# The opening and the close of a hybrid decoder layer: the norm's weights in four row tiles, filler matmuls, an earlier x tile, an earlier scale

## The chip, the core and the metric

The kernel runs on one core of a Trainium2 chip. The core has five engines that work at the same time: TensorE (PE, matmuls and transposes, writes to PSUM), VectorE (DVE), ScalarE (ACT), GpSimd (POOL) and SyncE (SP, which mostly issues transfers). The metric is the device time of one execution in microseconds (us).

## The reference

One layer: RMS norm of x (512 rows of 1024), one input projection, eight heads of block-sparse attention beside eight heads of a chunked gated delta rule, an output projection, and a squared-ReLU MLP, with a norm ahead of and behind each half. What the change touches is the first norm with the projection, and the last norm:

```
def rms_norm(x, w):
    xf = x.astype(jnp.float32)
    y = xf * lax.rsqrt(jnp.mean(xf * xf, axis=-1, keepdims=True) + EPS)
    return (y * w.astype(jnp.float32)).astype(x.dtype)
...
h = rms_norm(x, pre_mix_norm[l])
proj = jnp.einsum('bsd,dc->bsc', h, w_in[l])
...
x = x + rms_norm(mix, post_mix_norm[l])
h = rms_norm(x, pre_mlp_norm[l])
m = jnp.einsum('bsf,fd->bsd', jnp.square(jax.nn.relu(jnp.einsum('bsd,df->bsf', h, w_up[l]))), w_down[l])
x = x + rms_norm(m, post_mlp_norm[l])
```

The sum of the scan's heads runs over chunks of 64 rows and needs the inverse of a triangular matrix for each; the kernel computes it in blocks of 32 and merges them.

## The kernel before

**Numbers in two parts.** Most products are made of three matmuls: an operand is split into a rounded part (hi, a cast on ACT) and the rest (lo, a subtraction on DVE or POOL), and hi·hi, hi·lo and lo·hi are added up (`mm3`, line 141; `split`, line 109; `ended`, line 132, for weights). Plain float32 matmuls, which are slower, are used for transposes (`transpose`, line 80), for the norm's weights and in the scan.

**Order.** TensorE's instructions stand in an order that a planner in the program writes out. Generators (`pre_norm`, `projections`, `scan` and others) yield either the name of a mark or a waiting time, and the class `Weave` (line 28) runs the one of the lowest rank whose time has come. Its clock `now` goes forward with each matmul by the columns that it streams (`mm`, line 76). The waiting times stand in the table `WAIT` (line 20), the times at which x tiles may be transposed in `START` (line 24). The plan's clock only orders instructions; on the chip they wait by semaphores. During the first norm ACT, DVE and POOL keep program order too (line 190), and in the MLP SP as well.

**The opening.** `pre_norm` (line 187) takes x in four tiles of 128 rows. Tile by tile: ACT squares and sums a row (line 214), POOL makes the reciprocal root (`rstd_of`, line 167, two instructions), DVE multiplies x by the root and by the norm's weights (line 220), TensorE transposes the result in 8 blocks (line 231), and ACT and DVE split it into `hT_h` and `hT_l`. The norm's weights have to stand in all 128 partitions: they are loaded as one row of 1024 (line 200), and two matmuls with a column of ones (line 209) spread them over two PSUM banks `nb`, from which DVE reads them.

SP issues in this order: x tile 0, the norm's row, x tile 1, two blocks of projection weights, x tile 2, two blocks more, x tile 3, and small constants. POOL issues the identity matrix that the transposes need (line 201).

`ahead` steps the generator `projections` (line 249): its first two steps issue the loads of the weights of the first two items, its third splits the first item's. After tiles 0 and 1 the sum of squares and the scaling of tiles 2 and 3 follow on ACT, POOL and DVE (lines 235 to 241), with the split of the second item's weights between them. Then the first two items' matmuls for tiles 0 and 1 run, 24 each (line 272), then the transposes of tiles 2 and 3.

**PSUM.** There are eight banks in three groups: two `mm`, three `g`, three `a` (line 156). A new tile of a group takes the bank that has been free longest, and its first writer waits until the tile before it has had its last read. The first two projection items take the two `mm` banks (line 262).

**The middle.** When the triangular inverses are done (mark `inverse`, line 732), `scan` (line 735) is put into the plan. It issues eight transfers that bring the inverses' blocks back (lines 742 and 745), yields `WAIT["merge"]`, and then puts its first matmuls (32x32 tiles, line 754) into TensorE's order, between those of the projection. Behind the projections come the weights of the output projection (line 895).

**The close.** In the MLP's down projection the last eight steps are run for one tile at a time (line 1387). For each, `half` (line 1309) squares and sums the second half row on ACT and multiplies it by the norm's weights on DVE (line 1320); then `finish` (line 1329) calls `normed_y` (line 1324: a small addition on DVE, the root on POOL), multiplies by the root, adds x (line 1336) and issues the stores.

## Time and profile before

| | us |
|---|---|
| runs, median (lowest to highest) | 658.01 (657.56 to 658.2) |
| profiled execution, its own time | 657.88 |
| its span, first to last instruction | 656.1 |

The span is 1.8 us shorter than the execution's own time. The profile shows one execution. "Busy" is the time in which an engine had an instruction running; PE is TensorE's matmuls and PEld its weight loads, which overlap them. A timeline row gives the start, the duration, the engine, the line of the program, what is written and read with its shape, how many instructions the row merges, and in brackets how long the engine had been idle and what ended that. The chain of waits is followed back from the last instruction, at each step to what released it. A line can be a helper's: line 77 is every matmul, line 81 every transpose, and 134, 135, 110 and 111 are the halves of a split.

### The profile page before, as it was taken

To read this page: it belongs to the slowest core of one execution; us is meant where nothing else is said; L and a number is where in the kernel's file an instruction comes from. 1 tells how busy PE (TensorE), PEld (TensorE's weight loads), DVE (VectorE), ACT (ScalarE), POOL (GpSimd) and SP (SyncE) were. 2 spreads that over 40 slices of the span, in tenths; PEclk is the share of its full clock that TensorE was granted. 3 is DMA by queue.
4 is the path that set the end of the run, shared out by engine and by line. 5 is a ranking of instruction groups with operands and counts; after the bars stand their busy time and mean duration, and the time that the engine had idled before them with its cause. 6 is when DMAs were issued, how large, how long until landed. Compare 5 with 4: busy or idle time off the path is not lost.

```text
span 656.1 us, 11128 instructions
## 1 busy us (share of the span) xinstructions
PE 630.3 (96%) x4357; PEld 523.6 (80%) x4357; DVE 445.9 (68%) x643; ACT 358.9 (55%) x602; POOL 180.5 (28%) x215
## 2 busy tenths in 40 slices
PE   7899989989999999989999999999999999999995
PEld 4788767766677777668899899999998888887884
DVE  4358676897522364566455678888879888988775
ACT  6366463364646656744332576566565656665661
POOL 4356655422446234002402132111111230000002
PEclk9999999989999999999999999999999999999998
DMA  7132313223251202482278998999889999957503
GB/s 241 61 100 79 81 65 104 98 77 125 96 114 50 67 34 81 135 274 105 97 303 230 234 250 195 233 274 283 241 233 335 322 295 290 287 194 291 194 1 128
DMA packets 60225, 113.16 MB, mean 172 GB/s; under 512 B 15700, under 2 KB 34644, under 8 KB 59790
## 3 DMA queue, kind: packets, MB, share of 16 engines
q1 hardware_dynamic: 42446, 83.03, 36.3%
q0 software_dynamic: 17728, 29.43, 21.6%
q8 instruction: 34, 0.56, 0.4%
q14 instruction: 17, 0.14, 0.1%
HBM read 106.65 MB, written 35.15 MB: 216 GB/s over the span
## 4 chain that ended last, share of the span: by engine, by line
PE 82%; DVE 8%; DMA 6%; ACT 2%; issue 1%; POOL 1%; SPq 0%; DVEq 0%; POOLq 0%; ACTq 0%
PE ps_mm L77 43%; PE ps_g L77 22%; PE ps_a L77 14%; DMA w_raw<-in_w_out 3%; PE ps_a L81 2%; PE ps_g L81 1%; DVE inv L726 1%; DVE conv L346 1%; DVE pr L725 1%; DMA xx<-in_x 1%; DMA xy<-d_x 1%; DMA wd<-d_T 1%; DMA inv<-d_n 1%; DVE wo_l L123 1%; POOL rkq L172 0%
## 5 line engine op out<-in xcount | busy, mean ns | idle before, releaser
L135 POOL TENSOR_TENSOR w_lo<-w_raw,w_hi 128x512 fp32r<-128x512 f32 x54 | 70.6, 1308 | 119.2 <-ACT w_hi L134 111.3
L77 PE MATMUL ps_mm<-hT_h,w_hi 128*128 128x512 f32 (+1 forms) x224 | 94.0, 420 | 1.0 <-DVE conv L346 1.0
L77 PE MATMUL ps_mm<-hT_h,w_lo 128*128 128x512 f32 (+1 forms) x224 | 87.3, 390 | 0.0
L77 PE MATMUL ps_mm<-hT_l,w_hi 128*128 128x512 f32 (+1 forms) x224 | 87.2, 389 | 0.0
L110 ACT CAST wdh<-wd 128x1024 fp32r<-128x1024 f32 x53 | 55.8, 1053 | 52.2 <-PE ps_mm L77 23.6
L111 DVE TENSOR_TENSOR u_l<-w,u_h 128x1024 fp32r<-128x1024 f32 x46 | 56.2, 1224 | 36.0 <-ACT u_h L110 35.4
L111 DVE TENSOR_TENSOR wdl<-wd,wdh 128x1024 fp32r<-128x1024 f32 x53 | 64.9, 1225 | 22.9 <-ACT wdh L110 22.7
L110 ACT CAST u_h<-w 128x1024 fp32r<-128x1024 f32 x46 | 47.8, 1046 | 55.6 <-PE ps_a L77 20.7
L1133 POOL DMA_DIRECT2D d_T<-in_w_down x32 | 33.0, 1032 | 144.5 <-DMA d_T<-in_w_down 84.2
L134 ACT CAST w_hi<-w_raw 128x512 fp32r<-128x512 f32 x56 | 34.6, 619 | 42.6 <-PE ps_mm L77 17.1
L77 PEld LDWEIGHTS ps_mm<-hT_h,w_hi 128*128 128x128 f32 x224 | 43.1, 193 | 14.5 <-issue 7.2
L77 PEld LDWEIGHTS ps_mm<-hT_h,w_lo 128*128 128x128 f32 x224 | 43.1, 192 | 9.0
L168 POOL TENSOR_SCALAR s<-s 128x1 f32<-128x1 f32 x12 | 3.8, 317 | 167.5 <-DVE s L1326 108.6
L77 PEld LDWEIGHTS ps_mm<-hT_l,w_hi 128*128 128x128 f32 x224 | 43.3, 193 | 6.2 <-DVE hT_l L111 0.2
L77 PE MATMUL ps_mm<-wdh,u_h 128*128 128x512 f32 x116 | 45.3, 390 | 0.0
L77 PE MATMUL ps_mm<-wdl,u_h 128*128 128x512 f32 x116 | 45.2, 389 | 0.0
L77 PE MATMUL ps_mm<-wdh,u_l 128*128 128x512 f32 x116 | 45.1, 389 | 0.0
L346 DVE SCALAR_TENSOR_TENSOR conv<-ps_mm,cw,conv 128x511 f32<-128x511 f32 (+2 forms) x36 | 26.8, 744 | 12.5 <-ACT conv L343 12.1
L111 DVE TENSOR_TENSOR u_l<-f,u_h 128x1024 fp32r<-128x1024 f32 x28 | 34.1, 1219 | 0.0
L77 PE MATMUL ps_g<-wdh,u_h 128*128 128x512 f32 x80 | 31.2, 390 | 0.4 <-DVE y L1307 0.4
L77 PE MATMUL ps_g<-wdh,u_l 128*128 128x512 f32 x80 | 31.1, 389 | 0.0
L77 PE MATMUL ps_g<-wdl,u_h 128*128 128x512 f32 x80 | 31.1, 389 | 0.0
(428 smaller groups left out, 1725.8 us busy)
## 6 DMA issues: line engine op xcount, KB each, us to landing
d_T<-in_w_down POOLq DMA_DIRECT2D x48, 512.0 KB, 10.9
wd<-d_T SPq DMA_DIRECT2D x32, 512.0 KB, 6.2
w<-in_w_up SPq DMA_DIRECT2D x28, 512.0 KB, 8.0
w_raw<-in_w_in SPq DMA_DIRECT2D x54, 256.0 KB, 2.6
wd<-in_w_down SPq DMA_DIRECT2D x24, 512.0 KB, 8.1
w_raw<-in_w_out SPq DMA_DIRECT2D x16, 256.0 KB, 2.8
d_T<-d_T POOLq DMA_DIRECT2D x8, 512.0 KB, 11.9
xx<-in_x SPq DMA_DIRECT2D x4, 512.0 KB, 6.5
```

The lines of the kernel that those rows point to most:

```text
L77: nc.tensor.matmul(o, l, r, **kw)
L81: nc.tensor.transpose(o, i, ident[:k, :k])
L110: nc.scalar.copy(hi, src)
L111: tt(lo, src, f32(hi), op=OP.subtract)
L123: (sub or tt)(lo, raw, f32(hi), op=OP.subtract)
L134: nc.scalar.copy(hi, raw)
L135: (sub or tt)(lo, raw, f32(hi), op=OP.subtract)
L168: nc.gpsimd.tensor_scalar(r, ss, 1.0 / n, EPS, op0=OP.mult, op1=OP.add)
L346: stt(c[:, s:], p[:, :512 - s], cw[:, ft, j:j + 1], c[:, s:], op0=OP.mult, op1=OP.add)
L725: tt(v, iN[:, 0:m, m:m + 1].to_broadcast([128, m, w]), iU[:, m:m + 1, m:32].to_broadcast([128, m, w]), op=OP.mult)
L726: tt(iU[:, 0:m, m:32], iU[:, 0:m, m:32], v, op=OP.subtract)
L1133: nc.gpsimd.dma_start(d_T[t][k], block(b, second)[k], accum_op=OP.add, max_dma_last_dim=1024)
```

## The change

- The norm's weights are loaded as four rows of 256, into partitions 0, 32, 64 and 96, and spread by four matmuls of one row each at four row positions of the array, into four banks: three `a`, one `mm`. DVE's scaling of a tile becomes four instructions of 256 columns instead of two of 512.
- `busy(n)` puts n float32 matmuls of 128 columns on a tile of ones into TensorE's order, which write to the other `mm` bank and are read by nobody: six ahead of the norm's weights, five behind them, two between the transposes of tiles 0 and 1.
- SP issues the identity matrix, behind x tile 1 and ahead of the projection's weights, instead of POOL.
- At the close, `normed_y` is called for tiles 0 and 1 right behind the last sum of squares, ahead of the product with the norm's weights.
- `WAIT["merge"]` is 11.0 instead of 10.

```
-WAIT = {... 'merge': 10, ...}
+WAIT = {... 'merge': 11.0, ...}
+FILL = (6, 5, 2)
...
     def pre_norm(ahead):
-        one = tmp("one")[:1, :128]
-        nc.vector.memset(one, 1.0)
+        ones = tmp("one")
+        nc.vector.memset(ones[:, :128], 1.0)
...
-        nrow = nb0[:1]
         sqs = big("xs0", (128, 2, 1024))
-        nb = [bank("a") for _ in range(2)]
+
+        nb = [bank("a"), bank("a"), bank("a"), bank("mm")]
+        idle = bank("mm")
+
+        def busy(n):
+            for _ in range(n):
+                mm(idle[:, :128], ones[:, :128], ones[:, :128], start=True, stop=True)
...
         take(0)
-        nc.sync.dma_start(nrow[:, :1024], pre_mix[None, :])
-        nc.gpsimd.dma_start(ident, c_ident)
+        nc.sync.dma_start(nb0[0:128:32, :256], pre_mix.rearrange("(a b) -> a b", a=4))
         take(1)
+        nc.sync.dma_start(ident, c_ident)
         ahead()
...
-        for b in range(2):
-            mm(nb[b], one, nrow[:, 512 * b:512 * b + 512], start=True, stop=True)
+        busy(FILL[0])
+        for b in range(4):
+            mm(nb[b][:, :256], ones[32 * b:32 * b + 1, :128], nb0[32 * b:32 * b + 1, :256], start=True, stop=True, tile_position=(32 * b, 0))
+        weave.now -= 3 * 256 * 4 / 2400
+        busy(FILL[1])
         mark("x")
...
         def scaled(t, r):
-            for b in range(2):
-                bs = slice(512 * b, 512 * b + 512)
-                stt(sqs[:, t % 2, bs], xx[t // 2][:, t % 2, bs], r, nb[b], op0=OP.mult, op1=OP.mult)
+            for b in range(4):
+                bs = slice(256 * b, 256 * b + 256)
+                stt(sqs[:, t % 2, bs], xx[t // 2][:, t % 2, bs], r, nb[b][:, :256], op0=OP.mult, op1=OP.mult)
...
             mark(f"h{t}", WAIT["h"])
+            if t == 0:
+                busy(FILL[2])
             if t == 1:
...
         act(z, o, AF.Square, accum_out=ss[:, t, b:b + 1])
+        if b and t < 2:
+            normed_y(t)
         if b:
```

More of the change, by code (lines that the diff above doesn't have):

```diff
@@ L18 @@
 EPS = 1e-6
-WAIT = {'h': 1.7, 'conv_k': 5.5, 'k': 2.95, 'conv_q': 6.15, 'q': 4.5, 'conv_v': 11.0, 'v': 6.02, 'z': 7.99, 'ab': 0.1, 'g': 11.93, 'scalars': 3.68, 'r_in': 0.72, 'r_out': 4.4, 'kk': 2.46, 'kk_out': 14.43, 'gl': 2.12, 'qk': 3.88, 'va': 1.38, 'a': 2.4, 'row': 1.38, 'rows': 3.2, 'pv': 1.54, 'att': 1.3, 'inverse': 0.9, 'merge': 10, 'p1': 1.5, 'p2': 1.7, 'w': 1.78, 'vn': 1.0, 'state': 1.12, 'o_in': 3.6, 'o': 3.73, 'wo': 0.88, 'wo_out': 17.6, 'normed': 11.21, 'n': 1.7, 'up': 1.9, 'sums': 1.5, 'turned': 0.5, 'pv0': 1.5}
+WAIT = {'h': 1.7, 'conv_k': 5.5, 'k': 2.95, 'conv_q': 6.15, 'q': 4.5, 'conv_v': 11.0, 'v': 6.02, 'z': 7.99, 'ab': 0.1, 'g': 11.93, 'scalars': 3.68, 'r_in': 0.72, 'r_out': 4.4, 'kk': 2.46, 'kk_out': 14.43, 'gl': 2.12, 'qk': 3.88, 'va': 1.38, 'a': 2.4, 'row': 1.38, 'rows': 3.2, 'pv': 1.54, 'att': 1.3, 'inverse': 0.9, 'merge': 11.0, 'p1': 1.5, 'p2': 1.7, 'w': 1.78, 'vn': 1.0, 'state': 1.12, 'o_in': 3.6, 'o': 3.73, 'wo': 0.88, 'wo_out': 17.6, 'normed': 11.21, 'n': 1.7, 'up': 1.9, 'sums': 1.5, 'turned': 0.5, 'pv0': 1.5}
 RANK = {'chunks': 5, 'inverse': 3, 'scan': 3, 'scores': 5, 'values': 5, 'finish_o': 1, 'take': 4}
 LEAD = {'chunks': 0, 'inverse': 0, 'scan': 100, 'scores': 0, 'values': 100, 'finish_o': 0, 'take': 0, 'take_a': 100}
+FILL = (6, 5, 2)
 START = (5.5, 9.0, 17, 16, 30, 9.0)
```

## The prediction

> **What bounds the kernel now.** I read the page first, then the chain of waits at both ends, then the timeline of the opening and of the close.

> ```profile
> span 656.1 us, 11128 instructions
> PE 630.3 (96%) x4357; PEld 523.6 (80%) x4357; DVE 445.9 (68%) x643; ACT 358.9 (55%) x602; POOL 180.5 (28%) x215
> PE 82%; DVE 8%; DMA 6%; ACT 2%; issue 1%; POOL 1%; SPq 0%; DVEq 0%; POOLq 0%; ACTq 0%
> ```

> TensorE sets the time: 96% busy, 82% of the chain. So what the opening gains or loses is handed on to every matmul behind it, and the close counts by itself.

> ```profile
> 0.00:4.20 4.20, 0.00 (x0) 0.01 (x1) 0.23 (x3) 1.47 (x2) 1.07 (x6) 1.00 0.55 187
> 24.30:30.00 5.70, 5.68 (x33) 3.80 (x34) 0.00 (x0) 1.53 (x3) 0.56 (x1) 1.00 0.01 3
> ```

> These are busy times by stretch (PE is the first number after the length). PE does nothing for 4.2 us and is saturated from 24.3 on. Between them the chain goes:

> ```profile
> 1.55 5.81 DMA xx<-in_x
> ...
> 7.38 1.16 ACT xs L214 x2
> ...
> 8.89 0.56 POOL ss L172
> ...
> 9.48 1.41 DVE xs L220 x2
> 10.88 0.61 DVE hT_l L111
> ...
> 11.54 1.12 PE ps_g L81 x4
> 12.66 7.47 PE ps_mm L77 x48
> ```

> The second x tile lands at 7.36; call that X, 7.38 where ACT takes it up. Its square sum, root, scaling, VectorE's low half of tile 0 (over at 11.49: call that T), the last transposes, and then the 48 first projection matmuls follow one another.

> ```profile
> 1.55 0.35 SPq L197 DMA_DIRECT2D xx<-in_x  x1
> ...
> 4.01 1.06 ACT L214 ACTIVATE xs<-xx 128x1024 f32<-128x1024 f32 x1 [2.01 <-DMA xx<-in_x]
> ...
> 4.22 3.75 PE L77 MATMUL ps_a<-nb,one 1*128 1x512 f32 x4 [4.22 <-DMA nb<-in_pre_mix]
> ...
> 5.52 0.56 POOL L172 TENSOR_TENSOR ss<-ss,mhalf 128x1 f32<-128x1 f32 x1
> ...
> 12.69 0.59 ACT L110 CAST hT_h<-ps_g 128x512 fp32r<-128x512 f32 x1 [0.68 <-PE ps_g L81]
> ...
> 13.39 0.41 PE L77 MATMUL ps_mm<-hT_h,w_hi 128*128 128x256 f32 x1
> ...
> 13.60 0.41 PE L77 MATMUL ps_mm<-hT_l,w_hi 128*128 128x256 f32 x1
> ...
> 15.47 2.76 DVE L220 SCALAR_TENSOR_TENSOR xs<-xx,ss,ps_a 128x512 f32<-128x512 f32 x4
> ...
> 16.97 0.28 PE L77 MATMUL ps_mm<-hT_h,w_lo 128*128 128x256 f32 x1
> ...
> 17.09 0.28 PE L77 MATMUL ps_mm<-hT_h,w 128*128 128x256 f32 x1
> ```

> Two things stand here. Equal matmuls start 0.21 us apart at 13.4 and 0.12 apart at 17: PE runs the first third of the projection at about half rate, although the clock column above reads 1.00. And the second projection item begins at 17.09 (its operand is w instead of w_hi), while VectorE is still scaling x tiles 2 and 3, until 15.47+2.76 = 18.23. Today these two don't touch each other.

> **The change, part by part.** *The norm's weights.* Two one-row matmuls over 1024 columns take 3.75 us, 3.66 ns a column. Four row tiles of 256 columns cost 0.94 us if they run together and 3.75 if they run in turn. The nearest row for row tiles:

> ```profile
> 203.66 0.96 PE L77 MATMUL ps_a<-pt 64*128 64x512 f32 x6
> L400 DVE TENSOR_TENSOR vB<-ps_g,beta 128x256 f32<-128x256 f32 x8 | 3.1, 419 | 2.0 <-PE ps_g L81 2.0
> ```

> Six matmuls of 512 columns in two row halves took 0.96 us; in turn, at 0.24 (twice 0.12), they would take 1.44. So tiles overlap, and I take 0.94. The weights then stand at about 5.2, so the scaling of tile 0 waits only for its root, over at 5.52+0.56 = 6.08.

> The scaling itself pays: four pieces of 256 columns, at the 0.42 of the 256-column row, are 1.68 a tile against 1.41, so 0.27 more on each of four tiles.

> *The bank.* This is the step that I weigh most. The fourth quarter of the weights takes one of the two `mm` banks, and the fillers take the other. The first two projection items need just these two. The fillers' bank is free early; the other is held until VectorE has scaled tile 3. So the second item may no longer begin before that scaling ends: a new wait, with all of PE's queue behind it. Its place, worked out: now 18.23 = T + 1.17 (transposes up to 12.66) + 0.62 (cast, to 13.28) + 2.19 (to 15.47) + 2.76. After: the scaling is 8 x 0.42 = 3.36, and the transposes 0.56 less if PE is at full rate, which makes T + 6.78. And T = X + 2.10 + 1.68 + 0.61 = X + 4.39, but not before 6.08 + 2 x 1.68 + 0.61 = 10.05. The second item's shift is X + 11.17 − 17.09.

> *X.* The identity matrix goes from POOL's queue to SP's, behind the second x tile.

> ```profile
> GB/s 0 0 52 269 393 321 315 262 174 249 262 377 393 361 357 393 433 396 236 165 33 0 1 141 305 365 262 152 257 292 10 53 0 0 102 108 0 0 0 0
> ident<-in_c_ident POOLq DMA_DIRECT2D x1, 64.0 KB, 5.7
> ```

> These are rates in slices of 0.625 us over the first 25. At the 393 of the fifth slice, 512 KB take 1.33 us; ACT takes up the first tile at 4.01, so X could be 5.4 at best. At worst it stays at 7.38. Transfers of the weights and the identity run in the same stretch, of which only the identity leaves, so I take the middle, 6.4. Then T = 10.8, the wait ends at 17.6, and the second item is **0.5 us later** than now; X = 5.4 gives 0.25 earlier (16.83), X = 7.38 gives 1.46 later. SP's issue of the identity (about 0.35 us, as that of a tile at 1.55) stands ahead of the weights and of tiles 2 and 3. ACT and POOL take those up behind work that is later still; without that cover it is 0.35 us. POOL, freed of its issue, has nothing to do then.

> [...]

> *The fillers.* 128 columns at 3.66 ns are 0.47 us: six take 2.8 us inside the 4.2 in which PE does nothing, five take 2.3 behind the weights (5.2 to 7.5; half that at full rate), two stand between the transposes of tiles 0 and 1. Their price is nothing if the clock rises and PE waits for X anyway. If it doesn't rise, transposes of tile 0 start at 7.5, tile 1's end at about 12.5, as now. Whether it rises:

> ```profile
> 122.16:125.57 3.41, 2.42 (x11) 1.73 (x10) 3.34 (x8) 1.21 (x3) 0.39 (x1) 1.00 0.23 77
> 132.40:135.81 3.41, 1.72 (x10) 1.20 (x10) 3.34 (x11) 1.66 (x4) 0.26 (x1) 0.97 0.04 10
> 135.81:139.23 3.42, 3.42 (x13) 2.26 (x11) 3.42 (x8) 2.26 (x7) 1.02 (x1) 0.54 0.23 77
> ```

> The granted clock is the third number from the end. A stretch of 3.41 us with PE busy for 1.72 is followed by one at 0.54; one with 2.42 busy kept full clock; the fully busy one brings it back. Six fillers fill up to 2.8 of such a stretch, nearer to 2.42 than to 1.72, so I take full rate, bounded by half rate.

> [...]

> *The plan's clock.* The fillers advance the generator's clock, but the start times of the x tiles are absolute, so the order behind them is the old one up to one constant.

> *Merge, 10 to 11.*

> ```profile
> L742 SPq DMA_DIRECT2D uap<-d_t x4: 303/460/1887, 182.7 to 185.5; - x4
> ...
> DMA to landing us min/median/max: 2.3/3.2/3.5
> ...
> 192.40 2.21 PE L77 MATMUL ps_g<-uap,NT 32*32 32x32 f32 x128
> ...
> PE ps_mm L77 <- ACT wo_h L122: 1.7, 1, 1.7
> ```

> The blocks were there by 185.5+3.5 = 189.0, 3.4 us before PE used them at 192.4. Holding the scan one planned us longer puts one or two projection steps (three matmuls at 0.24, 0.7 us) ahead of it. That is order, not work; PE has no gap there. It can reach the later wait of 1.7 for output weights, by 1.4 either way. I take 0.

> *The close.*

> ```profile
> 648.41 0.39 PE L77 MATMUL ps_mm<-wd_hl,u_l 128*128 128x512 f32 x1
> ...
> 648.89 0.60 ACT L1318 ACTIVATE sq<-ps_mm 128x512 f32<-128x512 f32 x1 [4.75 <-PE ps_mm L77]
> ...
> 649.61 0.69 DVE L1320 SCALAR_TENSOR_TENSOR y<-ps_mm,nb 128x512 f32<-128x512 f32 x1 [0.26 <-ACT sq L1318]
> 650.22 0.15 DVE L1326 TENSOR_TENSOR s<-ssy 128x1 f32<-128x1 f32 x1
> ...
> 650.73 0.55 POOL L172 TENSOR_TENSOR s<-s,mhalf 128x1 f32<-128x1 f32 x1
> 651.32 1.42 DVE L1336 SCALAR_TENSOR_TENSOR y<-y,s,xy 128x512 f32<-128x512 f32 x2 [0.94 <-POOL s L172]
> ```

> The sum of squares and the root now come ahead of the 0.69 product: the small addition starts at 649.61 instead of 650.22, and the product runs under POOL's two steps. Gain 0.61, on the path. For the first tile it hides behind the second's matmuls.

> *Sum:* +0.48 − 0.61 + 0 = −0.1. The profiled execution took 657.88 (span 656.1), so 657.8; the median of the runs is 658.01, 0.13 higher: **657.9 us**.

> **Rivals.**

> 1. *x comes at full transfer speed and the later scan helps: 656.4.* X = 5.4 (−0.25), the close (−0.61) and one projection step taken off the 1.7 wait (−0.7) make −1.6. For it: 393 GB/s are reached in the slice where nothing else runs. Against it: the weights still run beside x.
> 2. *The clock stays at half rate: 659.4, slower.* Place: the transposes of tile 1 and the bank's wait behind them. T = 11.77 at X = 7.38, then 7.34: 19.11, 2.0 late, less 0.61. An earlier X doesn't save it, since PE then ends those transposes at 12.5 to 12.8 by itself. It decides if matmuls at 12 to 13 us still start 0.21 apart. For it: PE was busy from 4.22 on and still slow at 13.6. Against it: those were one-row matmuls and transposes; the fillers use all rows.
> [...]
> 4. *The row tiles run in turn, so that part doesn't do what it says: 659.0.* The weights end at 7.97, T = 7.97 + 3.36 + 0.61 = 11.94, the wait 18.7: +1.6, less 0.61. Against it: the 0.96 row.

> **How the numbers follow.** Chances: forecast 0.40, rivals 0.24, 0.22, 0.10 and 0.04. 0.2% is 1.3 us, about what a measurement of this kernel can tell from no change: faster means below 656.7, slower above 659.3. Rival 1 gives nearly all of faster, 0.25. Rival 2 gives slower, and the upper bound of merge on rivals 3 and 4 some more: 0.28. The rest, 0.47, is within. Low end: −0.25 − 0.61 − 1.0 (most of merge's 1.4) = 656.1; high end: +2.0 − 0.61 + 0.8 (half of merge's other side) = 660.2. The forecast alone, X from 5.4 to 7.38 with merge at 0, spans 657.1 to 658.9.

> **What would show it.** X: the first instruction of ACT's second square sum. Clock: the spacing of the first projection matmuls, 0.12 or 0.21. Bank: PE idle ahead of the second item, ended by VectorE's scaling at line 220's new form, with its first matmul near 17.6. Row tiles: about 1 us for four matmuls. Close: VectorE's last pair starting 0.6 us sooner behind PE's end. I am wrong if the second item starts before tile 3 is scaled, or if PE gaps between 190 and 310 move by over 1.4 us.

## The result, and the profile after

| | before | after |
|---|---|---|
| runs, median (lowest to highest) | 657.94 (656.12 to 658.84, 20 runs) | 659.45 (657.07 to 662.71, 20 runs) |
| profiled execution, its own time | 657.88 | 658.88 |
| its span | 656.1 | 656.8 |

The ratio is 1.0029, 95% interval 1.0017 to 1.004: the change made the kernel **slower by 0.29%**, 1.5 us at the median. The times of the changed kernel also spread more here: before they lie within 2.7 us of each other, after within 5.6. That the change makes the spread is not shown: on another chip the kernel before spread over 5.25 us in 29 runs, and the changed one over 5.13 in 12 (after_again, below). Long times go with a low granted clock. The nine runs of the changed kernel with a mean clock of 0.994 or more have a median of 658.4, the eight with 0.992 or less one of 660.6.

The opening, from the timeline of the changed kernel (start, duration, engine, line, what is written and read, number of merged instructions, idle time before and what ended it):

```profile
4.88 0.80 PE L78 MATMUL ps_a<-nb,one 1*128 1x256 f32 x3 [0.88 <-DMA nb<-in_pre_mix]
...
5.47 0.64 PE L78 MATMUL ps_a<-nb,one 1*128 1x256 f32 x3
...
6.05 2.50 PE L78 MATMUL ps_mm<-one 128*128 128x128 f32 x10
6.29 1.06 ACT L224 ACTIVATE xs<-xx 128x1024 f32<-128x1024 f32 x1 [1.01 <-DMA xx<-in_x]
...
12.77 0.28 PE L78 MATMUL ps_mm<-hT_h,w_lo 128*128 128x256 f32 x1
...
12.89 0.28 PE L78 MATMUL ps_mm<-hT_h,w_hi 128*128 128x256 f32 x1
...
15.28 0.28 PE L78 MATMUL ps_mm<-hT_h,w_lo 128*128 128x256 f32 x1
...
17.20 0.47 DVE L230 SCALAR_TENSOR_TENSOR xs<-xx,ss,ps_mm 128x256 f32<-128x256 f32 x1
...
17.82 0.36 PE L78 MATMUL ps_mm<-hT_h,w 128*128 128x256 f32 x1 [2.26 <-DVE xs L230]
...
25.11 0.39 PE L78 MATMUL ps_g<-hT_h,abw 128*32 128x512 f32 x1 [1.69 <-DVE two L455]
```

The row tiles overlap: all are over by 6.1, 1.2 us after 4.88. X, where ACT takes up the second x tile, is 6.29. The first item's matmuls stand 0.12 apart, so the clock is up. The first item is over at 15.56; then PE idles **2.26 us** until VectorE has read the last piece of the norm's weights out of the `mm` bank (17.20 + 0.47), and the second item starts at 17.82. The last row, the first matmul on the small weights `abw`, serves below as a mark for the end of the opening; in the profile before it is at 24.32.

The close of the changed kernel:

```profile
649.78 0.39 PE L78 MATMUL ps_mm<-wd_hl,u_l 128*128 128x512 f32 x1
...
650.99 0.16 DVE L1340 TENSOR_TENSOR s<-ssy 128x1 f32<-128x1 f32 x1 [0.85 <-ACT sq L1330]
651.07 0.69 DVE L1334 SCALAR_TENSOR_TENSOR y<-ps_mm,nb 128x512 f32<-128x512 f32 x1
...
652.10 1.41 DVE L1350 SCALAR_TENSOR_TENSOR y<-y,s,xy 128x512 f32<-128x512 f32 x2 [0.34 <-POOL s L173]
```

From the start of PE's last matmul to VectorE's last pair it takes 2.32 us (652.10 − 649.78); before, 2.91 (651.32 − 648.41).

So the opening stands 0.79 later at the mark (25.11 − 24.32) and the close is 0.59 shorter, which would be +0.2. The rest lies between. In this execution the granted clock changes at 10.15, 136.44, 139.86, 293.46, 296.87 and 655.27: 37, 1, 45, 1 and 105 times 3.41 us apart. These are windows of the changed kernel, cut in stretches of 3.41 us to within 0.04 of those changes (length, busy time and count of PE, PE's weight loads, VectorE, ScalarE, GpSimd; then granted clock, share of the DMA engines, GB/s). The clock's records begin with its first change, here at 10.15: ahead of that the column reads 1.00, though PE still runs at half rate (eight transposes take 1.91 us from 8.34, and 1.04 from 10.55).

```profile
6.74:10.16 3.42, 3.42 (x18) 3.42 (x18) 2.99 (x9) 2.48 (x5) 1.98 (x4) 1.00 0.94 347
...
13.57:16.98 3.41, 1.99 (x17) 1.78 (x15) 3.13 (x8) 1.91 (x5) 2.52 (x6) 1.00 0.67 205
16.98:20.40 3.42, 2.58 (x22) 2.61 (x22) 1.19 (x3) 0.00 (x0) 1.39 (x4) 1.00 0.41 136
...
290.08:293.50 3.42, 1.18 (x5) 0.40 (x3) 1.09 (x2) 0.62 (x1) 0.00 (x0) 0.99 1.02 396
293.50:296.91 3.41, 3.37 (x8) 2.70 (x9) 0.87 (x2) 1.36 (x3) 0.00 (x0) 0.51 0.52 178
```

and the rows beside them in the timeline, first of the kernel before, then of the changed one:

```profile
274.84 0.66 PE L81 MATMUL ps_g<-ident,ot 128*128 128x128 f32 x4 [1.09 <-DVE om L876]
...
292.93 0.49 PE L77 MATMUL ps_mm<-wo_h,ma_h 128*128 128x512 f32 x1 [1.72 <-ACT wo_h L122]
...
314.67 0.66 PE L81 MATMUL ps_a<-ident,xs 128*128 128x128 f32 x4 [0.58 <-DVE ma_l L111]
```

```profile
292.82 0.50 PE L78 MATMUL ps_mm<-wo_h,ma_h 128*128 128x512 f32 x1 [2.06 <-ACT wo_h L123]
...
316.12 0.66 PE L82 MATMUL ps_a<-ident,xs 128*128 128x128 f32 x4 [0.58 <-DVE ma_l L112]
```

The gap of 1.09 at 274 is gone: PE comes to the output weights earlier, so at 290.8 it waits longer for them, 2.06 instead of 1.72. The merge's new time is not what closed that gap, as the runs below show. The stretch in which that wait lies has PE busy for 1.18 us only, and the next runs at 0.51. The stretch of 13.57 to 16.98 lies so that only 1.4 us of the bank's wait fell into it; PE was busy for 1.99 and the clock stayed. The transposes behind the first output tile (`ma_l`, 316.12) are the second mark.

Theory A, from these two profiles: the bank's wait delays the second item and, where a stretch holds most of it, takes half the clock from the next one. Rival B: the clock is lost at 291 only, through merge 11. Rival C: the early warming itself makes the clock unsteady.

### The profile page after: what moved, and what is told of

Same layout as the page of the kernel before. It is cut to its first block, busy times and chain, and to the rows that moved or that the text cites. A ratio compares the mean times of both kernels' runs of the same rounds, so it can differ in the third digit from the quotient of the medians.

```text
span 656.8 us, 11195 instructions
## 1 busy us (share of the span) xinstructions
PE 632.4 (96%) x4387; PEld 527.9 (80%) x4387; DVE 447.6 (68%) x651; ACT 359.7 (55%) x602; POOL 180.2 (27%) x214
## 4 chain that ended last, share of the span: by engine, by line
PE 81%; DVE 8%; DMA 5%; ACT 3%; issue 1%; POOL 1%; DVEq 0%; POOLq 0%; SPq 0%; ACTq 0%
PE ps_mm L78 41%; PE ps_g L78 23%; PE ps_a L78 14%; DMA w_raw<-in_w_out 3%; PE ps_a L82 2%; PE ps_g L82 1%; DVE pr L737 1%; DVE inv L738 1%; DVE conv L358 1%; DVE wo_l L124 1%; DMA wd<-d_T 1%; DMA inv<-d_n 1%; DMA nb<-in_pre_mix 1%; ACT wo_h L123 1%; POOL rkq L173 0%
## 5 line engine op out<-in xcount | busy, mean ns | idle before, releaser
L111 ACT CAST wdh<-wd 128x1024 fp32r<-128x1024 f32 x53 | 55.9, 1054 | 52.0 <-PE ps_mm L78 23.5
L111 ACT CAST u_h<-w 128x1024 fp32r<-128x1024 f32 x46 | 47.8, 1047 | 55.6 <-PE ps_a L78 20.7
## 6 DMA issues: line engine op xcount, KB each, us to landing
d_T<-d_T POOLq DMA_DIRECT2D x8, 512.0 KB, 10.8
```

The source lines that it names most:

```text
L111: nc.scalar.copy(hi, src)
```

## The experiments

**Fillers in the bank's wait (fill_wait), the merge back (merge10), no bank held (two_rows), the merge alone (merge11).**

```
 for i, ps in enumerate(first):
+    if i and not t:
+        idle = bank("g")
+        for _ in range(8):
+            mm(idle[:, :128], ones_r[0][:, :128], ones_r[0][:, :128], start=True, stop=True)
+        weave.now -= 8 * 128 * 4 / 2400
```

Here `ones_r[0]` is the tile of ones, and the last line takes the fillers out of the plan's clock, so that the order of everything else stays.

> The changed kernel with eight matmuls of 128 columns, on the constant ones, written into a free transposing bank between the first and the second projection item (about 1.9 us of work at the spacing of 0.24); the second item still waits for VectorE to scale tile 3, so the delay of about 0.8 us in the profiled pair stays. Theory A (PE's idle 2.26 us ahead of the second item costs clock in many executions, on top of the delay): the times draw together to 657.0 to 659, mean granted clock 0.994 or more in nearly all, median 658.1 (before's 657.9 + 0.8 - 0.6), over 1 us under the changed kernel. Rival B (the clock is lost at the longer wait for the output weights at 291 us, which the merge's later due time makes): nothing changes, median 659.4, times up to 662. Rival C (the early warming of the clock or the chip's own scatter): nothing changes either.

```
-'merge': 11.0
+'merge': 10
```

> The changed kernel with the merge's due time back at 10; opening and close as changed. Theory A (clock lost behind the 2.26 us wait for the bank): the scatter stays, times from 657 to 662 with clocks of 0.987 to 0.996, median 659.4 or up to 1 us above that, since the reordered scan's own gain of about 1.1 us at 274 goes too. Rival B (clock lost at 291 us, behind the wait of 2.06 us that merge 11 makes of 1.72): the scatter goes, clock 0.994 and more in all, median 658.1 (657.9 + 0.8 - 0.6).

```
-nb = [bank("a"), bank("a"), bank("a"), bank("mm")]
-idle = bank("mm")
+nb = [bank("a"), bank("a")]
+idle = bank("a")
...
-nc.sync.dma_start(nb0[0:128:32, :256], pre_mix.rearrange("(a b) -> a b", a=4))
+nc.sync.dma_start(nb0[0:64:32, :512], pre_mix.rearrange("(a b) -> a b", a=2))
...
```

> The changed kernel with the norm's weights as two row tiles of 512 columns in two of the three a banks, scaled in two pieces a tile as before, and the fillers in the third a bank; both projection banks are free from the start. Merge 11 stays. The second item then waits for its weights and its transposes alone; PE's idle time ahead of it falls from 2.26 to well under 1 us. Theory A: no scatter, clock 0.994 and more, median 657.0 (657.9 - 0.6 for the close - 0.3 for the earlier start). Rival B: the scatter stays, clocks down to 0.987, median 658.6 (0.8 of delay less than 659.4). Rival C (the early warming): the scatter stays as well.

The kernel before with one number changed, `'merge': 11.0`:

> The kernel before with the merge's due time at 11 and nothing else. Theory A: the clock isn't touched; median 657.9, from 656.8 (the scan's gap of 1.09 at 274 gone) to 658.3. Rival B: the clock is lost at 291 us in many executions, times up to 661, median 659 or more.

The kernel before ran at a median of 658.29 on that chip.

| | median (lowest to highest) | ratio to before, 95% |
|---|---|---|
| fill_wait | 657.83 (655.25 to 660.82) | 1.0000 (0.9983 to 1.0016) |
| merge10 | 660.81 (657.55 to 662.08) | 1.0039 (1.0022 to 1.0055) |
| two_rows | 659.33 (656.99 to 660.9) | 1.0022 (1.0008 to 1.0037) |
| merge11 | 661.32 (657.0 to 661.92) | 1.0035 (1.0015 to 1.0054) |

The fillers take off what the change had cost, as A said, but the spread stays, which A had not. Without merge 11 the kernel isn't better, so B falls as the whole cause. And A fails on the last two: without the bank's wait the time should have been 657.0, and merge 11 alone should have done nothing; there it came out as B said. The profile of two_rows shows why:

```profile
22.89 0.40 PE L78 MATMUL ps_g<-hT_h,abw 128*32 128x512 f32 x1 [1.69 <-DVE two L455]
...
250.30 1.76 DVE L879 TENSOR_TENSOR ot<-ot,oss 128x512 f32<-128x512 f32 x1 [2.60 <-POOL oss L878]
252.09 0.87 DVE L853 TENSOR_TENSOR S<-S,ps_g 64x256 f32<-64x256 f32 x2
253.01 1.09 PE L78 MATMUL ps_g<-S,LWQ 128*64 128x128 f32 x16 [1.55 <-DVE S L853]
...
294.50 0.50 PE L78 MATMUL ps_mm<-wo_h,ma_h 128*128 128x512 f32 x1 [2.71 <-ACT wo_h L123]
```

and its windows around the mark:

```profile
19.86:23.27 3.41, 1.19 (x8) 0.67 (x7) 2.79 (x6) 1.67 (x4) 0.47 (x2) 1.00 0.13 38
23.27:26.69 3.42, 3.42 (x10) 1.37 (x8) 0.00 (x0) 0.00 (x0) 0.00 (x0) 0.50 0.02 5
```

Its opening comes out right up to the mark: that is at 22.89, 2.2 us ahead of the changed kernel's. But the wait of 1.69 ahead of the mark lies in a stretch with PE busy for 1.19 only, and right behind the mark a stretch runs at half rate. And at 250 VectorE runs a product (`ot`) ahead of the sum of the scan's state (`S`) that PE waits for, 1.55 us; in the changed kernel the sum comes first, at 250.65, and PE doesn't wait there. PE's order from 190 to 330 is the same in both: the scan's order on VectorE turned over, presumably because the framework makes it from its own estimates and the opening's estimated times moved by a little (one filler more turns it back, in two_fill below). merge11 has the same gap of 1.55, and a half-rate stretch behind its wait at 291. In two_rows PE waits 2.71 at 291, with a half-rate stretch behind it too.

The gap at 274 does not go with the merge: merge11, with the new order, still has it (1.15, at 275.15), and merge10, with the old one, hasn't. All three profiles with the old opening (before, merge11, close) have it, none of the others. In the profile before, ScalarE waited 1.63 us there, until 272.14, for a transfer of output weights, and VectorE took up the product that PE waits for (`om`) behind their split. Why that transfer was late only with the old opening stays open.

Hence theory D: what costs most is any stretch of 3.41 us with more than about half of it idle (1.18 and 1.19 us busy in the two shown), wherever it lies, and the changed kernel has one such place more than the kernel before, and a wider one at 291. If so, matmuls that do nothing in these places must bring the time back, with the order of all computing engines unchanged. Rival E: the time is lost to the order of the scan.

**Fillers where PE waits (fill_291, fill_all, two_fill), and the close alone (close).** For the waits at 24 and 291 us the fillers add zeros into a bank that is in use anyway:

```
+def keep(ps, n):
+    for _ in range(n):
+        nc.tensor.matmul(ps[:, :128], zero, zero, start=False, stop=False, skip_group_check=True)
...
 for k in (4, 5, 6, 7, 0, 1, 2):
+    if (t, b, k) == (0, 1, 2):
+        keep(part[t][0][b], 6)
```

> The changed kernel, in its own order, with six matmuls of 128 columns that add zeros into the open projection bank, put where PE waits 2.06 us for the last output weight (about 1.45 us of work inside that wait); the opening keeps its wait of 2.26. Theory D, formed after the first four runs: a stretch of 3.41 us in which PE idles for more than about 1.7 us is followed by one at half rate, and the changed kernel loses 2 us at 293 in most of its executions and 1.5 at 17 to 21 in some. Then the stretch at 293 goes: no half-rate stretch there in the profile, median 658.0, 1 to 1.5 us under the changed kernel's 659.4. Theory A (the opening's wait alone costs the clock): no change, 659.4. Rival E (the time is lost to the order of the scan, not to the clock): no change, 659.4.

fill_all has the fillers of fill_wait and of fill_291, and these:

```
 yield "h3"
+keep(kept[0], 5)
 for k in range(8):
```

`kept[0]` is the bank of the first projection item.

> The same with the eight matmuls ahead of the second projection item as well, and five that add zeros into the first projection bank where PE waits 1.69 us for the small weights at 24 us; the order is otherwise the changed kernel's. The second item still waits for the bank, so its delay of about 0.8 us stays. Theory D: at most the stretches of the first 8 us and the one at 136 (worth about 0.6) are left; times draw together, from 655 to 658.5, median 656.7, over 2.5 us under the changed kernel and about 1.3 under the kernel before. Theory A: 657.8, as with the fillers of the opening alone. Rival E: 659 or more, with all the more matmuls to run.

two_fill is two_rows with the fillers at 24 and 291 and one line more:

```
-FILL = (6, 5, 2)
+FILL = (6, 6, 2)
```

> Two row tiles of 512 columns in the a banks, so that no projection bank is held, with six start fillers instead of five behind the weights, which gives VectorE the changed kernel's order at 250 us again (sum of the state ahead of the product), and with the fillers at 24 and 291 us. Theory D: the bank's wait, the gap of 1.55 at 251 that the two-row kernel had, and the half-rate stretches go: median 655.8, times from 655 to 657.5, clear of both kernels. Theory A: 657.0. Rival E (the clock isn't what costs): 657.5 to 658.5, since the bank's 0.8 and the gap's 1.55 go in any case from 659.3.

```
 act(z, o, AF.Square, accum_out=ss[:, t, b:b + 1])
+if b and t < 2:
+    normed_y(t)
```

> The kernel before with the close alone (the root of the sum of squares taken ahead of the last product). All theories: 0.6 us off the end, median 657.7 where the kernel before has 658.3, and the same scatter as the kernel before, since nothing ahead of 640 us moves.

The kernel before had a median of 657.83 there.

| | median (lowest to highest) | ratio to before, 95% |
|---|---|---|
| fill_291 | 658.91 (657.06 to 660.18) | 1.0009 (0.9994 to 1.0025) |
| fill_all | 656.28 (655.05 to 656.65) | 0.9971 (0.9961 to 0.9981) |
| two_fill | 654.4 (653.01 to 655.5) | 0.9945 (0.9929 to 0.996) |
| close | 657.22 (656.28 to 659.36) | 0.9995 (0.9983 to 1.0006) |

fill_all does more work than the changed kernel, with its computing engines in the same order, and is faster than it by 0.58% (1.0029 against 0.9971; the intervals are far apart); its times lie within 1.6 us instead of 5.6. That speaks for D and against E as the whole cause; rival C falls too, since fill_all has the early fillers as well. Its times should be held against the kernel before on the same chip, which spread over 4.4 us. Part of the gain came at a place without fillers: the half-rate stretch at 136 us that both profiles of the changed kernel have is missing in those of fill_wait, fill_291 and fill_all, where the same wait is shared otherwise between two stretches (in the changed kernel's first profile its 1.70 us, over at 135.02, lie whole in the stretch from 133.03, busy for 1.71, and 136.44 to 139.86 runs at 0.50), and they reach the scan's first matmuls (`uap`) 168.9 to 169.0 us behind the mark instead of 169.5. fill_291 gains less than D said; by its times it is told apart neither from the kernel before nor from the changed one. Its profile, cut at its own stretches, shows where the rest went:

```profile
13.65:17.06 3.41, 1.49 (x13) 1.28 (x11) 3.33 (x8) 1.72 (x5) 2.61 (x5) 1.00 0.74 221
17.06:20.47 3.41, 2.77 (x13) 2.80 (x14) 1.00 (x3) 0.00 (x0) 1.20 (x3) 0.50 0.36 120
20.47:23.89 3.42, 3.42 (x18) 3.42 (x18) 0.00 (x0) 0.00 (x0) 0.48 (x2) 0.50 0.13 38
```

Two stretches at half rate follow the bank's wait, and the mark comes at 27.76. At 291 PE keeps its clock. In fill_all all three waits have shrunk, as the fillers now stand in them:

```profile
17.71 0.36 PE L78 MATMUL ps_mm<-hT_h,w 128*128 128x256 f32 x1 [0.84 <-DVE xs L237]
...
25.01 0.39 PE L78 MATMUL ps_g<-hT_h,abw 128*32 128x512 f32 x1 [0.57 <-DVE two L471]
...
291.26 0.49 PE L78 MATMUL ps_mm<-wo_h,ma_h 128*128 128x512 f32 x1 [0.21 <-ACT wo_h L123]
```

and two_fill has no wait for the bank at all:

```profile
15.29 0.28 PE L78 MATMUL ps_mm<-hT_h,w_lo 128*128 128x256 f32 x1
15.41 0.28 PE L78 MATMUL ps_mm<-hT_h,w 128*128 128x256 f32 x1
...
22.89 0.39 PE L78 MATMUL ps_g<-hT_h,abw 128*32 128x512 f32 x1 [0.57 <-DVE two L464]
```

The second item begins at 15.41, with no gap behind the first, and the sum on VectorE comes first again. two_fill beats both kernels by most, the one before by 0.55%. The close alone isn't told from no change by the times, and its 0.6 rests on the profiles: from the second mark (`ma_l`) to the end of the span it takes 341.4 us in the two without it (before, merge11) and 340.7 to 340.8 in the twelve with it.

**What the parts are worth there (two_nofill, two_ident, two_merge10), and the changed kernel once more (after_again).** The first three change one line each of two_fill: `FILL = (0, 0, 0)`; the identity issued by POOL; merge at 10.

> The kernel with two row tiles and fillers in the gaps (two_fill), without the fillers ahead of the first transposes; the order on all engines is otherwise the same. If the fillers warm the clock (prediction's forecast): full rate comes with the first stretch after the transposes have begun, 13.5 to 17 us by its phase, instead of 9.8, the first matmuls stand 0.21 apart, and the median is 1 to 1.6 us over two_fill's 654.4, with more scatter. [...]

> two_fill with the identity back on POOL's queue ahead of the second x tile. If the move to SP's queue is what brings the second tile of x forward (prediction: X 7.38 to 6.4; measured 6.29): ACT's second sum of squares starts at 7.2 to 7.4 again, and everything behind it is later by up to 1.0, median 655.3. If the queue makes no difference: X 6.3 to 6.5, median 654.4.

> two_fill with the merge's due time at 10, so the scan runs in the order of the kernel before. If merge 11 is worth its 1.1 to 1.4 us only by closing PE's gap at 274: that gap of about 1 us is back and the median is 655.6. If it is worth nothing (the prediction's value): 654.4.

> The changed kernel as it is, on the same chip as these three. Theory D: median 659.4 as before, times from 657 to 662.5, and in the profile, by the phase of its stretches, a half-rate stretch behind the bank's wait at 15.5 to 17.8, behind the weights' wait at 291 to 293, or both; the opening then stands 0.8 us late without and about 2.3 with the first.

| | median (lowest to highest) | ratio to before, 95% |
|---|---|---|
| two_nofill | 655.78 (653.35 to 657.17) | 0.9964 (0.9946 to 0.9983) |
| two_ident | 654.65 (653.49 to 656.87) | 0.9947 (0.9927 to 0.9967) |
| two_merge10 | 655.07 (653.86 to 656.49) | 0.9948 (0.9929 to 0.9967) |
| after_again | 660.23 (656.82 to 661.95) | 1.0028 (1.0008 to 1.0048) |

Beside two_fill's 0.9945, measured on another chip, none of the first three is told apart by its times; by the ratios they lie 1.2, 0.1 and 0.2 us higher. In two_nofill's profile PE is at half rate until 13.6, as forecast (equal matmuls start 0.21 apart up to there, 0.12 behind), but the second item starts at 15.63 instead of 15.41 and the mark is 0.2 later (23.09), so what the opening's fillers are worth stays open. In two_merge10 the gap at 274 did not come back; from mark to mark it takes 289.54 us, two_fill 288.74. That 0.8 is the merge's worth in one pair of profiles; the times don't show it. With the identity on POOL's queue X was 7.47, and what follows stood 0.5 later; but X is not steady. In the ten profiles with the identity on SP's queue it lies between 6.29 and 7.11, in the four with it on POOL's at 5.65, 7.38, 7.47 and 7.89. Whether the queue does it stays open.

The changed kernel's second profile fell on another cut of the stretches; its windows, and its rows beside them:

```profile
0.76:4.17 3.41, 2.93 (x12) 2.63 (x12) 0.23 (x3) 1.42 (x2) 0.07 (x1) 1.00 0.73 196
...
14.39:17.80 3.41, 1.13 (x10) 0.92 (x8) 3.41 (x9) 1.43 (x4) 2.61 (x5) 1.00 0.87 254
17.80:21.22 3.42, 3.06 (x14) 3.10 (x15) 0.71 (x2) 0.00 (x0) 1.39 (x5) 0.50 0.31 103
...
290.84:294.25 3.41, 2.08 (x10) 1.38 (x8) 2.75 (x5) 1.79 (x5) 0.00 (x0) 1.00 1.03 396
294.25:297.67 3.42, 2.60 (x10) 1.95 (x11) 0.69 (x1) 0.81 (x2) 0.00 (x0) 1.00 0.96 344
```

```profile
18.16 0.55 PE L78 MATMUL ps_mm<-hT_h,w 128*128 128x256 f32 x1 [2.64 <-DVE xs L230]
...
26.80 0.39 PE L78 MATMUL ps_g<-hT_h,abw 128*32 128x512 f32 x1 [1.69 <-DVE two L455]
...
294.84 0.49 PE L78 MATMUL ps_mm<-wo_h,ma_h 128*128 128x512 f32 x1 [1.92 <-ACT wo_h L123]
...
316.57 0.66 PE L82 MATMUL ps_a<-ident,xs 128*128 128x128 f32 x4 [0.58 <-DVE ma_l L112]
```

Same program, other places: here the clock is up from 4.17 already, the bank's wait lies almost whole in one stretch (1.13 busy) and the next is at half rate, while the wait at 291 is shared by two stretches and costs no clock. The mark of the opening is 1.69 later than in the first profile (26.80 − 25.11), half a stretch of 3.41. From mark to mark this one takes 289.77 (316.57 − 26.80), the first 291.01, the kernel before 290.35. So between the marks the changed kernel is 0.6 faster where it keeps its clock at 291, by the merge and the missing gap at 274 together, and the half-rate stretch at 293 cost 1.2.

## Why the prediction was wrong

The forecast was 657.9, no change that can be told. It came to 659.45, within the range of 656.1 to 660.2.

**The step that failed is "the bank".** Its place and cause were right: "a new wait, with all of PE's queue behind it", ended by VectorE's scaling, the second item at 17.6 (17.82 measured). Its price was wrong. It counted the delay of the second item alone, 0.48. The wait is also an idle time of 2.26 to 2.64 us, and where most of it fell into one stretch of 3.41 the next ran at 0.50 (1.13 us busy in after_again, 1.07 in merge10, 1.49 in fill_291). These are the second item's start and the mark in two more profiles of this opening, merge10 and then fill_291,

```profile
17.90 0.55 PE L78 MATMUL ps_mm<-hT_h,w 128*128 128x256 f32 x1 [2.47 <-DVE xs L230]
...
26.63 0.40 PE L78 MATMUL ps_g<-hT_h,abw 128*32 128x512 f32 x1 [1.69 <-DVE two L455]
...
17.70 0.55 PE L78 MATMUL ps_mm<-hT_h,w 128*128 128x256 f32 x1 [2.56 <-DVE xs L236]
...
27.76 0.39 PE L78 MATMUL ps_g<-hT_h,abw 128*32 128x512 f32 x1 [1.69 <-DVE two L461]
```

and in two of the old opening, merge11 and then close:

```profile
15.61 0.28 PE L77 MATMUL ps_mm<-hT_h,w 128*128 128x256 f32 x1
...
22.84 0.40 PE L77 MATMUL ps_g<-hT_h,abw 128*32 128x512 f32 x1 [1.69 <-DVE two L443]
...
17.98 0.28 PE L77 MATMUL ps_mm<-hT_h,w 128*128 128x256 f32 x1
...
25.20 0.40 PE L77 MATMUL ps_g<-hT_h,abw 128*32 128x512 f32 x1 [1.69 <-DVE two L443]
```

From the second item to the mark the old opening takes 7.2 us in all three profiles (merge11, before, close). The new one takes 7.29 where no half-rate stretch follows the wait (the changed kernel's first profile), 8.64 and 8.73 with one (after_again, merge10) and 10.06 with two (fill_291). So the lost clock cost nothing, 1.4 or 2.8 us on top of the delay. The rows that say so stood in the prediction, the stretch of 1.72 busy followed by 0.54; it used them for the fillers' benefit and not for the gap that it had just worked out.

**A second part of the same step: what it was measured against.** The prediction took the start of the second item before, 17.09, as fixed. In the three old profiles it is 15.61, 17.09 and 17.98, for two reasons. The second x tile is taken up at 5.65, 7.38 and 7.89, and the first item starts at 11.34, 12.31 and 12.82. And the first third of the projection runs at half rate until the clock's first change, at 13.7, 16.1 and 17.5, so that the first item takes 4.3, 4.8 and 5.2. The mean start is 16.9; that of the four new ones is 17.9. So the second item is on average 1.0 later, not 0.48, and with the lost clock the mark is about 2.5 later (means of 26.6 and 24.1), though the new opening has the clock up earlier (10.15 and 4.17 in the changed kernel's two profiles). In the changed kernel's first profile the first item runs at full rate from 11.8 and ends 1.5 us earlier than the 17.09 before; all of that, and more, is spent waiting for the bank. two_fill, without that wait, has the mark at 22.89.

**Merge, "I take 0".** It is worth about −0.8 between the marks in the one pair of profiles whose programs differ in nothing else (two_fill, two_merge10; taken on two chips), and the changed kernel waits longer at 291 (1.72 to 2.06), which turns into another half-rate stretch in some executions. The bound of 1.4 held it. That the same 11 costs time with the old opening (merge11: 0.35%) was not thought of: its profile takes 293.5 from mark to mark, 3.2 more than the kernel before, with the gap of 1.55 and the half-rate stretch at 294 in it.

**What held.** X, 6.4 (6.29, and 6.90 in the second profile); as X differs from execution to execution with either queue, that is in part luck. No run shows an X of 7.2 as what the identity's move leaves, the case to which 0.10 of the chances went; on SP's queue it was 7.11 at most. Row tiles together, 0.94 (1.2 measured at half rate, not 3.75). Full rate is there in time: matmuls at 12.8 stand 0.12 apart, so the second rival's place is refuted, though the result lies at its 659.4; it is the loss of the clock behind the gap, not a clock that never rose. The close, 0.61 (0.59).

The clock's stretches lie elsewhere from one execution to the next: counted back in steps of 3.41 us from the first change, they begin at 2.45 in the profile before, at 3.32 in the changed kernel's first and at 0.76 in its second. The second run of fillers joins the row tiles ahead of it and the transposes behind it: in the first profile PE is busy without a pause from 4.88, the stretch from 6.74 to 10.16 wholly, and full rate follows; in the second full rate came behind a stretch with only 2.93 us busy. Gaps of 2.47 to 2.64 us were followed by half rate (merge10, fill_291, after_again).

By the sums: −0.6 for the close, −0.6 between the marks and 2.5 for the opening on average (four profiles against three) make +1.3, and a share of the 1.2 at 291 comes on top; 1.5 and 1.9 were measured, on two chips. How large that share is stays open, as a profile shows one execution: the close's profile, with the old order, has a half-rate stretch at 294 as well.

## What to carry to other kernels

Price a new wait on TensorE twice: as a delay, and as idle time of PE. Here the five stretches of 3.41 us with PE busy for 1.07 to 1.49 were all followed by one at half rate, and such a one cost 1.2 to 1.4 us where its price could be read (both profiles of the changed kernel, merge10); that price counts for the share of executions in which the wait falls so. Matmuls that do nothing, put into that wait, are worth trying before anything else: here they brought back all that the change had lost, and more (fill_all, 656.28 against 657.83). A resource taken early for a small gain (a bank for a quarter of the weights) is to be followed to the next one who needs it, and a baseline whose transfers land and whose clock rises at other times in every execution (X from 5.65 to 7.89, the clock's first change from 13.7 to 17.5 in three) is a range, not a number.
